# Batch norm with ReLU: two channels per partition in 8 KB rows, and parameters loaded as rows instead of columns

## Chip, cores and metric

The kernel runs on one core of a Trainium2 chip. The metric is the device time of one execution in microseconds (us); the median of several executions is given. The profile is one execution under the hardware profiler; its span is 1.8 to 2.2 us shorter than that execution's time, because the time also holds what lies outside the program's first and last record.

## The reference

```python
# x: (32, 128, 32, 32) float32; gamma, beta, running_mean, running_var: (128,)
normalized = (x - running_mean[None, :, None, None]) / np.sqrt(running_var[None, :, None, None] + eps)
scaled = normalized * gamma[None, :, None, None] + beta[None, :, None, None]
return np.maximum(scaled, 0).astype(np.float32)
```

Per channel this is `relu(scale * x + bias)` with scale = gamma / sqrt(var + eps) and bias = beta - mean * scale. The kernel reads 16.78 MB and writes 16.78 MB.

## The kernel before

Channels lie on the 128 partitions. An image's channel is 4 KB in a row in memory, so a tile of two images is a 1 MB transfer of 256 pieces of 4 KB. Loads are issued from SP, stores from ACT.

```python
x_r = x.rearrange("b c h w -> c b (h w)")
plan = [(b0, 2, 0, HW) for b0 in range(0, B - 2, 2)]
plan += [(B - 2, 1, 0, HW), (B - 1, 1, 0, HW // 2), (B - 1, 1, HW // 2, HW // 2)]
HEAD = 8; BUFS = 12
# ... the first 8 loads are issued from SP ...
nc.scalar.dma_start(out=var_t, in_=running_var.unsqueeze(1))   # [128, 1]: one 4-byte piece per partition
nc.scalar.dma_start(out=gamma_t, in_=gamma.unsqueeze(1))
nc.scalar.dma_start(out=mean_t, in_=running_mean.unsqueeze(1))
nc.scalar.dma_start(out=beta_t, in_=beta.unsqueeze(1))
# ... sqrt on ACT, four small operations on DVE give scale_t and bias_t ...
for k, (b0, nb, h0, nh) in enumerate(plan):
    # ... from k = 8 on, the tile's load is issued here ...
    nc.scalar.activation(out=xt, in_=xt, func=relu, bias=bias_t, scale=scale_t)
    nc.scalar.dma_start(out=out_r[:, b0 : b0 + nb, h0 : h0 + nh], in_=xt)
```

## Time and profile before

| | before |
|---|---|
| time, median (13 runs) | 87.54 us (87.38 to 87.67) |
| span of the profile | 85.8 us |
| plateau of the transfers, 24 to 66 us | 421 GB/s |
| mean rate, 1 to 10 us | 284 GB/s |
| first activation, first store issued | 11.85 us, 13.97 us |
| ACT busy | 35.1 us |

The DMA row counts tenths of busy time of the 16 DMA engines in each fortieth of the span; the GB/s row says what they moved. A stretch line gives the stretch, its length, the busy time of each engine with the number of instructions in brackets, the TensorE clock, the share of the DMA engines (just over 1.00 where packets overlap) and GB/s as the last number.

### The profile page before, as it was taken

What the parts mean: (1) busy time and instruction counts of PE and PEld (TensorE: products, weight loads), DVE (VectorE), ACT (ScalarE), POOL (GpSimd) and SP (SyncE); (2) the same over time, 40 slices, a digit from 0 to 9 for tenths busy, and PEclk for the clock granted to TensorE, in tenths of its full rate; (3) what the DMA queues carried; (4) which work ended last, traced back from release to release, by engine and by line L of the source; (5) the groups of instructions that cost most, each with busy time, mean ns of one, the idle gap of its engine ahead of it and who ended that gap; (6) DMA issues with size and microseconds to landing.
All of it is one profiled execution on the core that took longest, in us unless ns stands there. A gap on an engine that the chain in (4) does not pass through costs nothing.

```text
span 85.8 us, 137 instructions
## 1 busy us (share of the span) xinstructions
DVE 0.7 (1%) x5; ACT 35.1 (41%) x20; POOL 0.2 (0%) x4
## 2 busy tenths in 40 slices
DVE  0000100000000000000000000000000000000000
ACT  0024047979749500791000098000098497710000
POOL 0000000000000000000000000000000000000000
DMA  3899999999999999999999999999999999999991
GB/s 29 214 352 333 407 420 413 401 424 422 420 415 424 424 422 416 418 428 422 415 418 426 424 420 415 422 426 424 415 416 428 415 417 421 422 422 413 424 407 55
DMA packets 9600, 33.56 MB, mean 391 GB/s; under 512 B 1152, under 2 KB 1152, under 8 KB 9600
## 3 DMA queue, kind: packets, MB, share of 16 engines
q1 hardware_dynamic: 4512, 16.78, 49.7%
q10 hardware_dynamic: 5088, 16.78, 48.1%
HBM read 16.78 MB, written 16.78 MB: 391 GB/s over the span
## 4 chain that ended last, share of the span: by engine, by line
DMA 72%; ACT 10%; ACTq 4%; issue 1%; DVE 0%; SPq 0%; DVEq 0%
DMA out_dram<-xt 34%; DMA xt<-in_x_dram 27%; DMA beta_t<-in_beta_dram 11%; ACT xt L82 10%; ACTq L83 2%; ACTq L56 1%; ACTq L57 1%; ACTq L55 1%; DVE bias_t L74 0%; SPq L81 0%; DVEq L74 0%
## 5 line engine op out<-in xcount | busy, mean ns | idle before, releaser
L82 ACT ACTIVATE xt<-xt,bias_t,scale_t 128x2048 f32<-128x2048 f32 (+2 forms) x18 | 33.5, 1899 | 34.4 <-DMA out_dram<-xt 10.2
L64 ACT ACT_TABLE_LOAD x1 | 1.3, 1283 | 5.9 <-DMA var_t<-in_running_var_dram 5.9
L64 ACT ACTIVATE std_t<-var_t,eps_t 128x1 f32<-128x1 f32 x1 | 0.3, 295 | 0.0
L66 DVE RECIPROCAL rstd_t<-std_t 128x1 f32<-128x1 f32 x1 | 0.2, 163 | 6.6 <-ACT std_t L64 6.6
L74 DVE TENSOR_TENSOR bias_t<-beta_t,tmp_t 128x1 f32<-128x1 f32 x1 | 0.2, 159 | 1.4 <-DMA beta_t<-in_beta_dram 1.4
L73 DVE TENSOR_TENSOR tmp_t<-mean_t,scale_t 128x1 f32<-128x1 f32 x1 | 0.2, 160 | 1.2 <-DMA mean_t<-in_running_mean_dram 1.2
L69 DVE TENSOR_TENSOR scale_t<-gamma_t,rstd_t 128x1 f32<-128x1 f32 x1 | 0.2, 159 | 1.2 <-DMA gamma_t<-in_gamma_dram 1.2
L100 POOL MEMSET const-bfloat16-1.0<- 128x1 bf16 x1 | 0.1, 102 | 0.0
L100 POOL MEMSET const-uint8-127<- 128x1 uint8 x1 | 0.1, 102 | 0.0
L100 POOL MEMSET const-float32-0.0<- 128x1 f32 x1 | 0.1, 99 | 0.2 <-issue 0.2
L100 POOL MEMSET const-float32-1.0<- 128x1 f32 x1 | 0.1, 99 | 0.0
L61 DVE MEMSET eps_t<- 128x1 f32 x1 | 0.1, 59 | 0.8 <-PEq L100 0.8
## 6 DMA issues: line engine op xcount, KB each, us to landing
xt<-in_x_dram SPq DMA_DIRECT2D x15, 1024.0 KB, 16.4
out_dram<-xt ACTq DMA_DIRECT2D x15, 1024.0 KB, 12.2
xt<-in_x_dram SPq DMA_DIRECT2D x1, 512.0 KB, 22.3
xt<-in_x_dram SPq DMA_DIRECT2D x2, 256.0 KB, 19.4
out_dram<-xt ACTq DMA_DIRECT2D x1, 512.0 KB, 10.0
out_dram<-xt ACTq DMA_DIRECT2D x2, 256.0 KB, 9.6
var_t<-in_running_var_dram ACTq DMA_DIRECT2D x1, 0.5 KB, 5.1
gamma_t<-in_gamma_dram ACTq DMA_DIRECT2D x1, 0.5 KB, 7.5
```

Of the source, the lines that this page charges most:

```text
L55: nc.scalar.dma_start(out=var_t, in_=running_var.unsqueeze(1))
L56: nc.scalar.dma_start(out=gamma_t, in_=gamma.unsqueeze(1))
L57: nc.scalar.dma_start(out=mean_t, in_=running_mean.unsqueeze(1))
L61: nc.vector.memset(eps_t, eps_f)
L64: nc.scalar.activation(out=std_t, in_=var_t, func=sqrt, bias=eps_t, scale=1.0)
L66: nc.vector.reciprocal(out=rstd_t, in_=std_t)
L69: nc.vector.tensor_mul(out=scale_t, in0=gamma_t, in1=rstd_t)
L73: nc.vector.tensor_mul(out=tmp_t, in0=mean_t, in1=scale_t)
L74: nc.vector.tensor_sub(out=bias_t, in0=beta_t, in1=tmp_t)
L82: nc.scalar.activation(out=xt, in_=xt, func=relu, bias=bias_t, scale=scale_t)
L83: nc.scalar.dma_start(out=out_r[:, b0 : b0 + nb, h0 : h0 + nh], in_=xt)
L100: nc = _bacc.Bacc("TRN2", target_bir_lowering=False, num_devices=1)
```

## The change

It has two intents. First, longer pieces: the tensor is viewed flat, and each partition takes 2048 neighbouring elements, which are two channels of one image, so a 1 MB transfer is 128 pieces of 8 KB. A partition then holds two channels and needs two scale and bias columns. Second, cheaper parameters: each vector comes as one contiguous row on one partition, issued from GpSimd, and small matmuls against a single 1.0 turn even and odd elements into columns. Besides, all eight 2 MB tiles have a buffer of their own. The diff, cut to its core:

```diff
-    x_r = x.rearrange("b c h w -> c b (h w)")
+    x_p = x.rearrange("b c h w -> (b c h w)").rearrange("(j p f) -> p j f", p=C, f=F)   # F = 2 * HW
-    data = ctx.enter_context(tc.tile_pool(name="data", bufs=BUFS))
+    data = ctx.enter_context(tc.tile_pool(name="data", bufs=NT))                        # NT = 8 tiles of 2 MB
+        eng = nc.sync
+        eng.dma_start(out=tiles[k][:, h], in_=x_p[:, 2 * k + h])
-    nc.scalar.dma_start(out=var_t, in_=running_var.unsqueeze(1))      # and three more
+    for nm, src in (("g", gamma), ("b", beta), ("m", running_mean), ("v", running_var)):
+        r = consts.tile([1, C], fp32, name=f"r{nm}")
+        nc.gpsimd.dma_start(out=r, in_=src.unsqueeze(0))
+        for t in range(2):
+            rows[(nm, t)] = r[:, t : C : 2]
+        nc.tensor.matmul(out=p[0:C2], lhsT=r, rhs=ones1)              # for each of the eight rows
+        nc.tensor.matmul(out=p[C2:C], lhsT=r, rhs=ones1)
     # ... the constants' chain now runs twice, for t = 0 and 1 ...
-        nc.scalar.activation(out=xt, in_=xt, func=relu, bias=bias_t, scale=scale_t)
-        nc.scalar.dma_start(out=out_r[:, b0 : b0 + nb, h0 : h0 + nh], in_=xt)
+        for t in range(2):
+            nc.scalar.activation(out=xt[:, :, t * HW : (t + 1) * HW], in_=xt[:, :, t * HW : (t + 1) * HW],
+                                 func=relu, bias=bias_c[t], scale=scale_c[t])
+        for h in range(2):
+            seng = nc.scalar
+            seng.dma_start(out=out_p[:, 2 * k + h], in_=xt[:, h])
```

More of the change, by code (lines that the diff above doesn't have):

```diff
@@ L25 @@
     HW = H * W
-    assert C == nc.NUM_PARTITIONS, f"expected C == 128, got {C}"
-    x_r = x.rearrange("b c h w -> c b (h w)")
-    out_r = out.rearrange("b c h w -> c b (h w)")
+    C2 = C // 2
+    F = 2 * HW
+    x_p = x.rearrange("b c h w -> (b c h w)").rearrange("(j p f) -> p j f", p=C, f=F)
+    out_p = out.rearrange("b c h w -> (b c h w)").rearrange("(j p f) -> p j f", p=C, f=F)
+    g2 = gamma.rearrange("(cp t) -> t cp", t=2)
+    b2 = beta.rearrange("(cp t) -> t cp", t=2)
+    m2 = running_mean.rearrange("(cp t) -> t cp", t=2)
+    v2 = running_var.rearrange("(cp t) -> t cp", t=2)
     eps_f = float(eps)
@@ L34 @@
     sqrt = mybir.ActivationFunctionType.Sqrt
-    plan = [(b0, 2, 0, HW) for b0 in range(0, B - 2, 2)]
-    plan += [(B - 2, 1, 0, HW), (B - 1, 1, 0, HW // 2), (B - 1, 1, HW // 2, HW // 2)]
-    HEAD = 8
-    BUFS = 12
-    data = ctx.enter_context(tc.tile_pool(name="data", bufs=BUFS))
-    consts = ctx.enter_context(tc.tile_pool(name="consts", bufs=1))
-    head_tiles = []
-    for k in range(HEAD):
-        b0, nb, h0, nh = plan[k]
-        xt = data.tile([C, nb, nh], fp32, tag="xt")
-        head_tiles.append(xt)
-        nc.sync.dma_start(out=xt, in_=x_r[:, b0 : b0 + nb, h0 : h0 + nh])
@@ L51 @@
-    var_t = consts.tile([C, 1], fp32)
-    gamma_t = consts.tile([C, 1], fp32)
-    mean_t = consts.tile([C, 1], fp32)
-    beta_t = consts.tile([C, 1], fp32)
-    nc.scalar.dma_start(out=var_t, in_=running_var.unsqueeze(1))
-    nc.scalar.dma_start(out=gamma_t, in_=gamma.unsqueeze(1))
-    nc.scalar.dma_start(out=mean_t, in_=running_mean.unsqueeze(1))
-    nc.scalar.dma_start(out=beta_t, in_=beta.unsqueeze(1))
+    NB = 2
+    NT = B // (2 * NB)
+    data = ctx.enter_context(tc.tile_pool(name="data", bufs=NT))
@@ new lines, with b0, load @@
+    consts = ctx.enter_context(tc.tile_pool(name="consts", bufs=1))
+    ppool = ctx.enter_context(tc.tile_pool(name="ppool", bufs=1, space=bass.MemoryType.PSUM))
+    tiles = [data.tile([C, NB, F], fp32, name=f"xt{k}", tag="xt") for k in range(NT)]
+    def b0(k, h):
+        return (2 * k + h) * NB
+    def load(k, h):
+        eng = nc.sync
+        eng.dma_start(
+            out=tiles[k][:, h],
+            in_=x_p[:, 2 * k + h],
+        )
+    load(0, 0)
+    load(0, 1)
+    rows = {}
+    for nm, src in (("g", gamma), ("b", beta), ("m", running_mean), ("v", running_var)):
[3 more added lines that the diff above has]
+            rows[(nm, t)] = r[:, t : C : 2]
@@ L60 @@
+    load(1, 0)
+    load(1, 1)
+    for k in range(2, NT):
+        load(k, 0)
+        load(k, 1)
+    ones1 = consts.tile([1, 1], fp32)
+    nc.vector.memset(ones1, 1.0)
+    cols = {}
+    for key, r in rows.items():
+        p = ppool.tile([C, 1], fp32, name=f"p{key[0]}{key[1]}")
+        nc.tensor.matmul(out=p[0:C2], lhsT=r, rhs=ones1)
+        nc.tensor.matmul(out=p[C2:C], lhsT=r, rhs=ones1)
+        cols[key] = p
     eps_t = consts.tile([C, 1], fp32)
     nc.vector.memset(eps_t, eps_f)
-    std_t = consts.tile([C, 1], fp32)
@@ L64 @@
-    nc.scalar.activation(out=std_t, in_=var_t, func=sqrt, bias=eps_t, scale=1.0)
-    rstd_t = consts.tile([C, 1], fp32)
-    nc.vector.reciprocal(out=rstd_t, in_=std_t)
-    scale_t = consts.tile([C, 1], fp32)
-    nc.vector.tensor_mul(out=scale_t, in0=gamma_t, in1=rstd_t)
-    bias_t = consts.tile([C, 1], fp32)
-    tmp_t = consts.tile([C, 1], fp32)
-    nc.vector.tensor_mul(out=tmp_t, in0=mean_t, in1=scale_t)
-    nc.vector.tensor_sub(out=bias_t, in0=beta_t, in1=tmp_t)
-    for k, (b0, nb, h0, nh) in enumerate(plan):
-        if k < HEAD:
-            xt = head_tiles[k]
-        else:
-            xt = data.tile([C, nb, nh], fp32, tag="xt")
-            nc.sync.dma_start(out=xt, in_=x_r[:, b0 : b0 + nb, h0 : h0 + nh])
-        nc.scalar.activation(out=xt, in_=xt, func=relu, bias=bias_t, scale=scale_t)
-        nc.scalar.dma_start(out=out_r[:, b0 : b0 + nb, h0 : h0 + nh], in_=xt)
+    scale_c = {}
@@ new lines @@
+    bias_c = {}
+    for t in range(2):
+        std = consts.tile([C, 1], fp32, name=f"std{t}")
+        nc.scalar.activation(out=std, in_=cols[("v", t)], func=sqrt, bias=eps_t, scale=1.0)
+        rstd = consts.tile([C, 1], fp32, name=f"rstd{t}")
+        nc.vector.reciprocal(out=rstd, in_=std)
+        sc = consts.tile([C, 1], fp32, name=f"sc{t}")
+        nc.vector.tensor_mul(out=sc, in0=cols[("g", t)], in1=rstd)
+        tmp = consts.tile([C, 1], fp32, name=f"tmp{t}")
+        nc.vector.tensor_mul(out=tmp, in0=cols[("m", t)], in1=sc)
+        bi = consts.tile([C, 1], fp32, name=f"bi{t}")
+        nc.vector.tensor_sub(out=bi, in0=cols[("b", t)], in1=tmp)
+        scale_c[t] = sc
+        bias_c[t] = bi
@@ new lines @@
+    for k in range(NT):
+        xt = tiles[k]
+        for t in range(2):
+            nc.scalar.activation(
+                out=xt[:, :, t * HW : (t + 1) * HW],
+                in_=xt[:, :, t * HW : (t + 1) * HW],
+                func=relu,
+                bias=bias_c[t],
+                scale=scale_c[t],
+            )
+        for h in range(2):
+            seng = nc.scalar
+            seng.dma_start(
+                out=out_p[:, 2 * k + h],
+                in_=xt[:, h],
+            )
```

## The prediction

> **What bounds the kernel now.** I read the page's first two parts first, then the stretches, then the waits. Engine work is small: the busiest engine is ACT with 35.1 us of 85.8. The DMA row is at nine tenths in all slices but the first two and the last.
>
> ```profile
> span 85.8 us, 137 instructions
> DVE 0.7 (1%) x5; ACT 35.1 (41%) x20; POOL 0.2 (0%) x4
> ...
> DMA  3899999999999999999999999999999999999991
> GB/s 29 214 352 333 407 420 413 401 424 422 420 415 424 424 422 416 418 428 422 415 418 426 424 420 415 422 426 424 415 416 428 415 417 421 422 422 413 424 407 55
> DMA packets 9600, 33.56 MB, mean 391 GB/s; under 512 B 1152, under 2 KB 1152, under 8 KB 9600
> ```
>
> The reader is to see a plateau near 421 GB/s, a ragged start (29, 214, 352, 333), and a short end (55). The stretches (columns: stretch, length, DVE, ACT, POOL, clock, DMA share, GB/s) give these in numbers.
>
> ```profile
> 1.00:10.00 9.00, 0.32 (x2) 1.58 (x2) 0.00 (x0) 1.00 0.89 284
> ...
> 24.00:66.00 42.00, 0.00 (x0) 16.27 (x8) 0.00 (x0) 1.00 1.03 421
> ```
>
> All bytes at the plateau rate are 33.55 MB / 421 GB/s = 79.7 us. The span is 85.8, so 6.1 us are lost at the two ends. At the start, 284 GB/s x 9 us = 2.56 MB have moved by 10.0 us, which would take 6.1 us at 421: 3.9 us lost. At the end some 2.2 us remain: the last bytes move near 84.0 us, and the rest is the landing of the last store. The kernel is therefore a DMA stream, and only three things can shorten it: the plateau rate, the start, the end.
>
> The start in half-microsecond stretches:
>
> ```profile
> 1.50:2.00 0.50, 0.00 (x0) 0.00 (x0) 0.00 (x0) 1.00 1.44 115
> 2.00:2.50 0.50, 0.00 (x0) 0.00 (x0) 0.00 (x0) 1.00 0.13 16
> 2.50:3.00 0.50, 0.00 (x0) 0.00 (x0) 0.00 (x0) 1.00 0.80 295
> 3.00:3.50 0.50, 0.00 (x0) 0.00 (x0) 0.00 (x0) 1.00 1.02 344
> 3.50:4.00 0.50, 0.00 (x0) 0.00 (x0) 0.00 (x0) 1.00 1.17 180
> 4.00:4.50 0.50, 0.00 (x0) 0.00 (x0) 0.00 (x0) 1.00 0.69 164
> ...
> 7.50:8.00 0.50, 0.15 (x1) 0.00 (x0) 0.00 (x0) 1.00 0.81 295
> ```
>
> The loads begin to flow at about 2.4 us (first issue at 0.73 us). That part is latency and stays. After it the rate should be flat, but it falls to 180 and 164 at 4 us and to about 300 near 7.5 us, while the four parameter vectors are under way. They land 5.1 (variance), 7.5, 8.3 and 9.3 us after their issue, as the DMA issues show, though each is 0.5 KB. From 2.5 to 10.0 us 2.49 MB moved, worth 5.9 us of 7.5: the dips cost 1.6 us. The load queue's own waits add that issues of x tiles wait for those vectors:
>
> ```profile
> SPq L49 <- DMA var_t<-in_running_var_dram: 3.6, 1, 3.6
> SPq L49 <- DMA mean_t<-in_running_mean_dram: 2.9, 1, 2.9
> ```
>
> No data dependence explains this, so I read it as transfers of all queues taking turns in a small set of completion counters. The first store leaves at 13.97 us, but from 10 to 14 us the loads alone already give 419 GB/s, so a late first store costs nothing.
>
> **What the Trainium skill says.** All four places are in the page "DMA: Bandwidth & Descriptors".
> (1) Section "Where 436 GB/s comes from": 16 ports of 32 B at 850 MHz give 435.2 GB/s. The trace agrees: its plateau of 421 is 97% of that, so at most 2.5 us of 79.7 can come from the rate.
> (2) Section "Why small descriptors are slow (HBM only)": a fixed overhead of about 3 cycles per packet. For 4 KB that is 131 cycles for 128, or 425 GB/s; for 8 KB 259 for 256, or 430: an estimate of +1.2%. The trace agrees in direction: the last two stores have rows of 2 KB, and from 82.5 to 83.5 us, where they drain, the rate is 381 and 410, mean 395.
> (3) Section "Specifications": pieces under 512 B make the DMA read, modify and write. The trace has 1152 such packets. 640 are one completion on each of 16 engines for 40 transfers; the other 512 are the four vectors, one element per partition. The dips stand where these are queued, which agrees; the trace does not show their cause.
> (4) Section "Anatomy of one DMA — SWDGE (gpsimd) path": about 2.0 us fixed for a transfer issued by GpSimd. No such transfer is in this trace.
>
> **The change part by part.**
> *Rows of 8 KB.* Two neighbouring channels of one image now go to one partition, so a 1 MB transfer is 128 rows of 8 KB in place of 256 of 4 KB. The bytes are unchanged and so is the number of 1 MB transfers, apart from the 512 and 256 KB ones at the end, which become one. Per engine a 4 KB packet takes 4096 / (421/16) = 155.7 ns, a 2 KB one 2048 / (395/16) = 83.0 ns. The line through the two is 10 ns per packet plus 72.7 ns per 2 KB, which makes 301 ns for 8 KB, or 435 GB/s: the skill's ceiling, so surely too much. Its own overhead gives 421 x 1.012 = 426. I take the middle of 421 and 435: 428 GB/s, hence 33.55 / 428 = 78.4 us, 1.3 us saved. All of it is on the path, because the stream is the path.
>
> *Parameters.* The four column loads on the ACT queue become four contiguous 512 B rows from GpSimd, so 512 four-byte pieces go. Of the 1.6 us that the dips cost I expect 1.2 us back; something will be left of it, since four small transfers and the first big ones still compete. New beside it: 16 small matmuls which turn the rows into columns, a doubled constant chain (two square roots, ten DVE operations of 0.16 us instead of four: about 1 us more), all beside loads that run anyway. An estimate for the first activation: four GpSimd issues of some 1 us, 2 us to land, 0.5 us of matmul, 1.28 us table load, 0.3 us square root and some 1 us of DVE, so about 10 us against 11.85 now. Neither is on the path.
>
> *ACT.* 15 activations of 2048 elements (2.09 us) and three smaller become 16 of two strided pieces of 1024, about 16 x 2.09 = 33.4 us, against 33.5 now. Sixteen store issues of 0.38 us add 6.1. ACT needs 39.5 us of 80.
>
> *Buffers.* Eight tiles of 2 MB hold the whole input, so no load needs a buffer that a store has to free. Before, loads waited long for stores, but the stream stayed at 421, so removing this wait is worth nothing by itself. The tile of 2 MB delays the first store by one activation, which also costs nothing.
>
> *Sum.* 87.5 - 1.3 (rate) - 1.2 (start) = 85.0 us. The end keeps its 2.2 us.
>
> **The rivals.**
> (a) *The rows don't matter*: the hardware cuts them to 4 KB or the plateau is bound elsewhere. For: 421 is already close to the ceiling. Against: the 2 KB stretch is slower, and single packets seem to follow the row length. It makes 87.5 - 1.2 = 86.3 us, within 2%.
> (b) *The start doesn't improve*: the dips belong to the first loads, or the GpSimd transfers bring their own delay. For: the dip at 4 us also falls where only the first three loads had been issued. Against: tiny packets are queued just there. It makes 86.2.
> (c) *ACT or the counters become the bound.* With 2 MB per step, ACT gives 2 MB in 2 x 2.09 + 2 x 0.38 = 4.9 us, and stores alone drain 2 MB in 5.0 us. If loads finish first with nothing computed ahead, small gaps appear. Transfers that take turns in shared counters can also hold a load behind a store. Against: before, the last activation ended at 75.4 us with 8 us of stores still queued, and ACT has 40 us to spare; constants could come some 25 us later without an effect. With a gap of 2 to 3 us it makes 87 to 88.
> (d) *Both gains at full size*: 435 GB/s and all of the dips: 87.5 - 2.5 - 1.6 = 83.4.
>
> **Range and chances.** Two per cent faster is 85.76 us. The middle estimate of 85.0 lies 0.8 us below it; either gain failing alone puts the time just above, 86.2 to 86.3. I give both gains about two in three of arriving at near their size or one at more than it. The range 83.5 to 86.9 us goes from (d) to a case where one fails and a small gap appears. Slower needs both to fail and (c) to cost over 4 us: 0.03.
>
> **What would show it.** Right: about half as many data packets (4096, beside the small ones); a plateau of 426 to 430 in the stretches; no dips to 180 after 2.5 us, so over 2.8 MB moved by 10 us; no parameter landing later than about 8 us; DMA at nine tenths to the end; ACT idle for half of the time. Wrong: a plateau of 421 with 8 KB rows breaks the first step; dips at the same places without the column loads break the second; slices under nine tenths in the middle, ended by waits for a landing or for ACT, would make (c) true.

## More of the kernel before

```profile
10.00:16.00 6.00, 0.32 (x2) 3.67 (x2) 0.00 (x0) 1.00 1.03 414
16.00:22.00 6.00, 0.00 (x0) 5.54 (x4) 0.00 (x0) 1.00 1.02 417
```

Both are close to the plateau: in this kernel the stores join without a visible loss.

## The result

| | before | after |
|---|---|---|
| time, median | 87.54 us (13 runs) | 85.36 us (8 runs, 85.04 to 85.68) |
| span of the profile | 85.8 us | 83.5 us |
| plateau, 24 to 66 us | 421 GB/s | 428 GB/s |
| 1 to 10 us | 284 GB/s | 355 GB/s |
| 10 to 16, 16 to 22 us | 414, 417 GB/s | 427, 365 GB/s |
| first activation, first store issued | 11.85, 13.97 us | 10.34, 14.45 us |

The ratio is 0.9752 (95% interval 0.9737 to 0.9768), so the kernel is faster by 2.5%. A ratio is the mean time of one kernel's runs over the mean of the other's runs in the same rounds; it is not quite the ratio of the medians in the table. Executions over 1.5% slower than the fastest of the same kernel are left out of the means. In a second set of rounds (e1 below) the same kernel had 0.9799: this kernel's advantage is known to about half a per cent only, and the second set alone would not settle whether it passes 2%.

The page of the changed kernel, parts 1 to 3:

```profile
span 83.5 us, 191 instructions
...
DMA  4799999999999999999999999999999999999992
GB/s 63 294 424 409 432 420 432 408 318 397 408 424 440 436 424 420 424 432 436 424 420 424 432 436 424 424 420 432 436 432 428 408 432 436 436 424 412 428 436 98
DMA packets 4736, 33.56 MB, mean 402 GB/s; under 512 B 640, under 2 KB 640, under 8 KB 640
```

There are 4736 packets where 9600 were. 640 are small, so 4096 are data packets of 8 KB: the hardware does not cut the rows. The ragged start is shorter. But slices nine and ten now read 318 and 397, where before had 424 and 422, and the DMA row shows nine tenths there all the same. Its stretches (a PE and a PEld column now stand ahead of DVE):

```profile
1.00:10.00 9.00, 2.19 (x32) 1.97 (x32) 0.59 (x5) 1.74 (x3) 2.06 (x4) 1.00 0.93 355
10.00:16.00 6.00, 0.00 (x0) 0.00 (x0) 0.43 (x4) 4.67 (x3) 0.00 (x0) 1.00 1.01 427
16.00:22.00 6.00, 0.00 (x0) 0.00 (x0) 0.00 (x0) 5.47 (x3) 0.00 (x0) 1.00 0.96 365
24.00:66.00 42.00, 0.00 (x0) 0.00 (x0) 0.00 (x0) 18.52 (x9) 0.00 (x0) 1.00 1.01 428
```

The start gains and the plateau gains, as predicted. The third line is new: from 16 to 22 us the engines are busy for 0.96 of the time but move only 365 GB/s. They mostly do not wait for work: single packets take longer. At its worst a half microsecond moves 279:

```profile
17.00:17.50 0.50, 0.00 (x0) 0.00 (x0) 0.00 (x0) 0.50 (x2) 0.00 (x0) 1.00 0.89 279
```

The first store is issued at 14.45 us, so the dip begins some 2 us after it. The trace also keeps each packet's start, length and size (the views print only their sums). By these records the load packets from 16 to 22 us take 358 ns on average and up to 721, where they take 309 from 24 to 66 us; the store packets take 309 as ever. The slow load packets start at 16.4 us, and the first store packet only at 18.3 us: 36 of the 56 that are more than a tenth too long start before it (in e3, further down, 58 of 59). So the dip follows the issue of the first store, but for the most part no stored byte moves yet. "When stores join" stands for this stretch from here on.

Where the time went, in microseconds of the plateau rate (lost = length - length x rate / plateau). Rate: 33.55 MB at 428 instead of 421 GB/s, 79.7 - 78.4 = 1.3 us gained. From 1 to 10 us: before lost 9 x (1 - 284/421) = 2.9, after 9 x (1 - 355/428) = 1.5; 1.4 us gained. From 10 to 22 us: before lost 0.16, after 6 x (1 - 427/428) + 6 x (1 - 365/428) = 0.90; 0.7 us given back. That makes 2.0 us of the 2.3 by which the span is shorter; the other 0.3 us was not taken apart.

### The profile page after: what moved, and what is told of

Read it like the earlier page. It is cut to its first block, busy times and chain, and to the rows that moved or that the text cites. A ratio compares the mean times of both kernels' runs of the same rounds, so it can differ in the third digit from the quotient of the medians.

```text
span 83.5 us, 191 instructions
## 1 busy us (share of the span) xinstructions
PE 2.2 (3%) x32; PEld 2.0 (2%) x32; DVE 1.1 (1%) x10; ACT 34.5 (41%) x19; POOL 2.3 (3%) x8
## 2 busy tenths in 40 slices
DMA packets 4736, 33.56 MB, mean 402 GB/s; under 512 B 640, under 2 KB 640, under 8 KB 640
## 3 DMA queue, kind: packets, MB, share of 16 engines
q1 hardware_dynamic: 2304, 16.78, 49.2%
q10 hardware_dynamic: 2304, 16.78, 47.6%
## 4 chain that ended last, share of the span: by engine, by line
DMA 70%; ACT 8%; issue 3%; POOL 1%; ACTq 1%; PE 1%; DVE 1%; POOLq 0%
DMA xt<-in_x_dram 46%; DMA out_dram<-xt 18%; ACT xt L108 8%; DMA rm<-in_running_mean_dram 7%; ACTq L117 1%; POOL rg L65 1%; PE pm L82 1%; ACT std L93 1%; POOL rb L65 1%; DVE tmp L99 0%; DVE sc L97 0%; PE pv L82 0%; DVE bi L101 0%; PE pv L83 0%; DVE rstd L95 0%
## 5 line engine op out<-in xcount | busy, mean ns | idle before, releaser
L108 ACT ACTIVATE xt<-xt,bi,sc 128x2048 f32<-128x2048 f32 x16 | 32.7, 2088 | 29.5 <-DMA xt<-in_x_dram 19.9
L82 PE MATMUL pg<-ones,rg 1*64 1x1 f32 x4 | 0.6, 239 | 6.7 <-DMA rg<-in_gamma_dram 6.7
L82 PEld LDWEIGHTS pg<-ones,rg 1*64 1x64 f32 x4 | 0.5, 210 | 6.7 <-issue 6.7
L65 POOL DMA_DIRECT2D rg<-in_gamma_dram x1 | 0.6, 619 | 0.8 <-POOLq L137 0.8
L82 PE MATMUL pb<-ones,rb 1*64 1x1 f32 x4 | 0.6, 246 | 0.3 <-DMA rb<-in_beta_dram 0.3
L83 PE MATMUL pb<-ones,rb 1*64 1x1 f32 x4 | 0.6, 246 | 0.0
L82 PE MATMUL pm<-ones,rm 1*64 1x1 f32 x4 | 0.6, 246 | 0.1
L83 PE MATMUL pg<-ones,rg 1*64 1x1 f32 x4 | 0.6, 246 | 0.0
L83 PE MATMUL pm<-ones,rm 1*64 1x1 f32 x4 | 0.6, 246 | 0.0
L82 PE MATMUL pv<-ones,rv 1*64 1x1 f32 x4 | 0.6, 240 | 0.0
L83 PE MATMUL pv<-ones,rv 1*64 1x1 f32 x4 | 0.6, 240 | 0.0
L82 PEld LDWEIGHTS pv<-ones,rv 1*64 1x64 f32 x4 | 0.5, 219 | 0.0
L83 PEld LDWEIGHTS pv<-ones,rv 1*64 1x64 f32 x4 | 0.5, 219 | 0.0
L82 PEld LDWEIGHTS pb<-ones,rb 1*64 1x64 f32 x4 | 0.5, 209 | 0.3 <-DMA rb<-in_beta_dram 0.3
L82 PEld LDWEIGHTS pm<-ones,rm 1*64 1x64 f32 x4 | 0.5, 208 | 0.2 <-DMA rm<-in_running_mean_dram 0.2
L83 PEld LDWEIGHTS pb<-ones,rb 1*64 1x64 f32 x4 | 0.5, 209 | 0.0
L83 PEld LDWEIGHTS pm<-ones,rm 1*64 1x64 f32 x4 | 0.5, 208 | 0.0
L83 PEld LDWEIGHTS pg<-ones,rg 1*64 1x64 f32 x4 | 0.5, 208 | 0.0
```

Of the source, the lines that this page charges most:

```text
L65: nc.gpsimd.dma_start(out=r, in_=src.unsqueeze(0))
L82: nc.tensor.matmul(out=p[0:C2], lhsT=r, rhs=ones1)
L83: nc.tensor.matmul(out=p[C2:C], lhsT=r, rhs=ones1)
L108: nc.scalar.activation(out=xt[:, :, t * HW : (t + 1) * HW], in_=xt[:, :, t * HW : (t + 1) * HW], func=relu, bias=bias_c[t], scale=scale_c[t],)
```

## The experiments

All runs gave correct results, each timed in five rounds beside the kernel before; the runs of one set share those rounds. Sets: e1 to e4, e5 to e8, e9 to e11, e12. The table gives what the stretches say. "Start" is the mean rate from 1 to 10 us with the time lost in it, "stores join" the time lost from 10 to 22 us, both against that kernel's plateau.

| kernel | time us (ratio to before) | plateau | start GB/s (lost us) | stores join, lost us |
|---|---|---|---|---|
| before | 87.54 | 421 | 284 (2.9) | 0.16 |
| after | 85.36 (0.9752) | 428 | 355 (1.5) | 0.90 |
| e1 after, again | 85.69 (0.9799) | 428 | 346 (1.7) | 0.93 |
| e2 four columns added | 86.62 (0.9914) | 428 | 295 (2.8) | 0.15 |
| e3 before, parameters only | 87.12 (0.9961) | 421 | 340 (1.7) | 0.90 |
| e4 after, 4 KB pieces | 87.04 (0.9956) | 421 | 329 (2.0) | 0.81 |
| e5 rows from ACT | 85.90 (0.9808) | 428 | 358 (1.5) | 1.12 |
| e6 one row more from ACT | 86.04 (0.9824) | 427 | 338 (1.9) | 0.72 |
| e7 one late transfer from ACT | 85.87 (0.9810) | 427 | 348 (1.7) | 0.77 |
| e8 stores from SP | 85.13 (0.9717) | 425 | 350 (1.6) | 0.04 |
| e9 one column added, ACT | 86.12 (0.9837) | 428 | 295 (2.8) | -0.06 |
| e10 second load from ACT | 85.34 (0.9751) | 428 | 360 (1.4) | 0.79 |
| e11 four columns added, GpSimd | 86.41 (0.9897) | 427 | 278 (3.1) | 0.10 |
| e12 16 KB pieces | 86.62 (0.9893) | 432 (66 to 80 us) | 353 (1.6) | 0.13 |

The plateau is that of 24 to 66 us, except for e12. For e8, the losses of the first ten microseconds and of the joining are against 428 GB/s, the plateau of the same pieces in e1; for e12 they are against its 66 to 80 us, as its 24 to 66 us hold a dip of their own. In those two the stores come behind all loads, near 42 us, so their last column shows loads alone.

### e1: the changed kernel again

No edit.

> The changed kernel unaltered, for a second profile and as the yardstick of this round: 85.4 us, ratio 0.975. In the first profile the rate fell to 279-344 GB/s from 16.5 to 19.5 us, worth 0.9 us, just before the first store's packets move. If this dip belongs to the kernel (stores joining the loads), it stands at the same place again. If it is a disturbance of one execution, it is elsewhere or gone, and that profile's span is some 0.9 us shorter.

85.69 us, and its stretches from 10 to 22 us:

```profile
10.00:16.00 6.00, 0.00 (x0) 0.00 (x0) 0.73 (x7) 4.34 (x3) 0.00 (x0) 1.00 1.00 423
16.00:22.00 6.00, 0.00 (x0) 0.00 (x0) 0.00 (x0) 5.80 (x3) 0.00 (x0) 1.00 1.01 367
```

The dip is back at the same place with the same size. It belongs to the kernel.

### e2: the column loads put back beside the rows

```diff
+    for nm, src in (("v", running_var), ("g", gamma), ("m", running_mean), ("b", beta)):
+        extra = consts.tile([C, 1], fp32, name=f"col{nm}")
+        nc.scalar.dma_start(out=extra, in_=src.unsqueeze(1))
```

> The changed kernel with the four column loads of before put back on the ACT queue beside the new row loads; their results are not used, so only their traffic is added. Theory (column loads make the dips of the start): dips to under 200 GB/s return near 4 us, 1 to 10 us falls from 355 to near 290 GB/s, time +1.2 to +1.5 us, 86.6 to 86.9 us. Rival (the dips came from the 4 KB rows or from the first loads alone): 85.4 us, the start stays at 350 or more.

86.62 us, 0.93 us more than e1 in the same rounds. The mean of the first ten microseconds fell as expected (without dips under 200 near 4 us: after 3 us the lowest half microsecond moves 246), but the last line was not expected by anybody:

```profile
1.00:10.00 9.00, 2.06 (x30) 1.85 (x32) 0.00 (x0) 1.28 (x1) 2.05 (x4) 1.00 0.81 295
...
16.00:22.00 6.00, 0.00 (x0) 0.00 (x0) 0.00 (x0) 5.52 (x3) 0.00 (x0) 1.00 1.02 427
```

So the columns do slow the start (295 against 346 in e1, 1.1 us), and with them the dip at the first stores is gone (427 against 367, 0.8 us). Of the 0.93 us that the time grew, the two together explain 0.3. The span of the profile grew by only 0.5 us (84.4 against 83.9), so some 0.4 us lie outside the program's records; the rest the stretches do not show.

### e3: the kernel before with only its parameters changed

```diff
-    nc.scalar.dma_start(out=var_t, in_=running_var.unsqueeze(1))      # and three more
+    for nm, src in (("g", gamma), ("b", beta), ("m", running_mean), ("v", running_var)):
+        r = consts.tile([1, C], fp32, name=f"r{nm}")
+        nc.gpsimd.dma_start(out=r, in_=src.unsqueeze(0))
+        p = ppool.tile([C, 1], fp32, name=f"p{nm}")
+        nc.tensor.matmul(out=p, lhsT=r, rhs=ones1)
```

> The kernel before with only its parameters changed: contiguous rows from GpSimd and four matmuls in place of the four column loads; 4 KB rows and the plan of transfers stay. Theory (two separate gains, 1.3 us of rate and 1.5 us of start): plateau stays 421 GB/s, start gains 1.5 us: 86.0 us. Rival (the start gains nothing without 8 KB rows): 87.5 us.

87.12 us, only 0.33 below before: neither theory. The start did gain, and the gain was lost again:

```profile
1.00:10.00 9.00, 1.99 (x8) 1.85 (x8) 0.35 (x3) 1.53 (x2) 2.05 (x4) 1.00 0.91 340
10.00:16.00 6.00, 0.00 (x0) 0.00 (x0) 0.29 (x2) 5.18 (x3) 0.00 (x0) 1.00 1.02 382
16.00:22.00 6.00, 0.00 (x0) 0.00 (x0) 0.00 (x0) 5.54 (x4) 0.00 (x0) 1.00 1.00 397
```

Its first store is issued at 12.48 us, earlier than in e1, and the dip came earlier with it: it straddles 16 us and costs 0.90 us, against 0.16 in before. The pieces are 4 KB here, so 8 KB rows are not what makes the dip.

### e4: the changed kernel in 4 KB pieces

```diff
-    tiles = [data.tile([C, NB, F], fp32, name=f"xt{k}", tag="xt") for k in range(NT)]
+    tiles = [data.tile([C, 2, NB, HW], fp32, name=f"xt{k}", tag="xt") for k in range(NT)]
-            out=tiles[k][:, h],
-            in_=x_p[:, 2 * k + h],
+            out=tiles[k][:, :, h],
+            in_=x_p[:, 2 * k + h].rearrange("p (t f) -> p t f", t=2),
```

The activations and stores follow the same layout.

> The changed kernel with the tile laid out so that the two channels of an image are not neighbours on a partition: the same addresses in memory, the same 1 MB transfers and order, but pieces of 4 KB. Theory (a fixed cost per packet sets the rate): 8192 data packets, plateau back from 428 to 421 GB/s, time +1.3 us, 86.7 us. Rival (the rate comes from the new order of addresses or from the free buffers): plateau 428, 85.4 us.

87.04 us, 1.35 us more than e1. Packets and plateau:

```profile
DMA packets 8832, 33.56 MB, mean 394 GB/s; under 512 B 640, under 2 KB 640, under 8 KB 8832
...
24.00:66.00 42.00, 0.00 (x0) 0.00 (x0) 0.00 (x0) 18.51 (x9) 0.00 (x0) 1.00 1.03 421
```

Same addresses, order and buffers, twice as many packets: the plateau is back at 421. The theory stands, with its size: 1.3 us expected, 1.35 measured (the two intervals leave about 0.2 us either way).

### e5, e6, e7: is the dip the first use of ACT's queue?

In before and e2 ACT issues the columns at the start; in the kernels with a dip ACT issues nothing before the first store. So a new theory: the first use of ACT's DMA queue disturbs the stream. Three edits use that queue earlier:

```diff
 e5: the four rows from ACT
-        nc.gpsimd.dma_start(out=r, in_=src.unsqueeze(0))
+        nc.scalar.dma_start(out=r, in_=src.unsqueeze(0))
 e6: one unused row more, from ACT, at the start
+    early = consts.tile([1, C], fp32, name="early")
+    nc.scalar.dma_start(out=early, in_=gamma.unsqueeze(0))
 e7: one small transfer from ACT that waits for the last row (8.7 us)
+    late = consts.tile([1, C], fp32, name="late")
+    nc.scalar.dma_start(out=late, in_=rv)
```

> The changed kernel with its four parameter rows issued from ACT in place of GpSimd. Theory (the first use of ACT's DMA queue disturbs the loads that run for some 3 us, wherever it falls; the changed kernel moved it from the start, where the stream is not yet up, to the first store, where it costs 0.9 to 1.0 us): no dip from 16 to 20 us, first 10 us at 340 or more since only 16 pieces of 32 B per row go, time 84.5 to 84.8 us. Rival (the dip belongs to the first stores, or to loads in flight): the dip stays, 85.6 us.

> The changed kernel with one more 512 B row load, unused, issued from ACT at the start. Theory (first use of ACT's queue): one such transfer is enough, no dip when the stores start, 84.5 to 84.8 us. Rival (first stores): nothing changes, 85.6 us. If e5 gains and this doesn't, it is not the first use but the GpSimd transfers that make the dip.

> The changed kernel with one small transfer from ACT that waits for the last parameter row, so ACT's queue is first used near 8.5 us, in the middle of the loads and 6 us before the first store. Theory: the dip of some 0.4 MB moves to about 10 to 14 us, none at 16 to 20, time as the changed kernel's, 85.4 to 85.7 us. Rival (first stores): the dip stays at its place after the first store's issue.

85.90, 86.04 and 85.87 us: no gain in any of them, and the dip stayed, 1.12, 0.72 and 0.77 us. In e7 the loads run undisturbed after the early use, 426 GB/s from 10 to 16 us, and dip only when stores are issued:

```profile
10.00:16.00 6.00, 0.00 (x0) 0.00 (x0) 1.03 (x8) 5.17 (x5) 0.00 (x0) 1.00 1.02 426
16.00:22.00 6.00, 0.00 (x0) 0.00 (x0) 0.00 (x0) 4.99 (x4) 0.00 (x0) 1.00 1.02 373
```

The test has a hole. ACT's queue in e6 shows 2306 packets, two more than the 2304 of e1, a data piece and its completion, so it seems that only one of the 16 engines was touched; e5 shows 2312, so one piece per row and not the 16 that its theory counted on; e7 shows 2336, that is one piece and one completion on each of the 16:

```profile
q10 hardware_dynamic: 2306, 16.78, 47.1%
```

The theory could be saved as "the first transfer on that queue with many pieces per engine". That is what e9 to e11 test.

### e8: stores from SP

```diff
-            seng = nc.scalar
+            seng = nc.sync
```

> The changed kernel with its stores issued from SP behind all loads, so that ACT issues no transfer at all and stores begin only when the loads are done. Theory: no dip of 0.4 MB anywhere before 40 us, and none where the stores begin, as SP's queue is long in use: 84.5 us, if one queue keeps the stream as full as two. Rival (first stores): a dip of 0.9 us where stores begin, 85.6 us or more.

85.13 us, ratio 0.9717 (0.9693 to 0.9742), the lowest. SP issues all loads first, so stores move only when the loads are through. The dip is gone:

```profile
10.00:16.00 6.00, 0.00 (x0) 0.00 (x0) 0.63 (x6) 5.44 (x3) 0.00 (x0) 1.00 1.02 430
16.00:22.00 6.00, 0.00 (x0) 0.00 (x0) 0.00 (x0) 6.00 (x4) 0.00 (x0) 1.00 1.01 423
24.00:66.00 42.00, 0.00 (x0) 0.00 (x0) 0.00 (x0) 19.71 (x10) 0.00 (x0) 1.00 1.01 425
```

The gain is smaller than the 0.9 us of the dip, as the plateau is 425 instead of 428 (422 from 24 to 40 us, where only loads move; 428 from 44 to 66 us, where only stores do). This run avoids the meeting of running loads with stores almost altogether, so it doesn't tell the queue from the stores. It was timed in other rounds than e1; against the changed kernel's 0.9752 and 0.9799 it is likely the better kernel, but the two were not run side by side.

### e9, e10, e11: which earlier transfer takes the dip away?

```diff
 e9: one unused column, 128 pieces of 4 B, from ACT
+    early = consts.tile([C, 1], fp32, name="early")
+    nc.scalar.dma_start(out=early, in_=gamma.unsqueeze(1))
 e10: the second 1 MB load from ACT
-        eng = nc.sync
+        eng = nc.scalar if (k, h) == (0, 1) else nc.sync
 e11: the four unused columns of e2, from GpSimd
-        nc.scalar.dma_start(out=extra, in_=src.unsqueeze(1))
+        nc.gpsimd.dma_start(out=extra, in_=src.unsqueeze(1))
```

> The changed kernel with one unused column load (128 pieces of 4 B, eight on each engine) issued from ACT at the start. New theory, since one piece on one engine or on each engine did not help: the dip belongs to the first transfer on ACT's queue that has many pieces per engine, and the four column loads of before took it at the start. Then no dip, or a much smaller one, from 16 to 20 us, and the first 10 us lose some of it: 300 to 340 GB/s, time 85.0 to 85.9 us. Rival (only large stores, or all four columns, matter): dip of 0.9 us unchanged, time 85.9 us or more.

> The changed kernel with its second 1 MB load issued from ACT: no traffic added, ACT's queue is in full use from the start. New theory: no dip where the stores begin, start at 340 GB/s or more, 84.6 to 85.0 us. Rival (stores joining from a second queue make the dip, whatever it did before): dip unchanged, 85.6 us.

> The changed kernel with the same four unused column loads as in e2, issued from GpSimd. It has the 512 small pieces, but ACT's queue is not used before the first store and no counter of the loads is taken. If the small pieces themselves slow the loads: first 10 us near 295 to 310 GB/s and the dip at the stores stays, 86.6 us. If the start of e2 was lost to ACT's queue and to the counters: start near 345, dip at the stores stays, 85.7 us.

e9, 86.12 us: one column is enough to slow the start, and no dip follows.

```profile
1.00:10.00 9.00, 1.80 (x28) 1.66 (x30) 0.00 (x0) 1.28 (x1) 2.05 (x4) 1.00 0.85 295
...
16.00:22.00 6.00, 0.00 (x0) 0.00 (x0) 0.00 (x0) 5.45 (x3) 0.00 (x0) 1.00 1.02 433
```

e10, 85.34 us: a full 1 MB load has gone through ACT's queue early, and the dip is there all the same.

```profile
1.00:10.00 9.00, 2.31 (x32) 2.04 (x32) 0.00 (x0) 1.41 (x2) 2.05 (x4) 1.00 0.91 360
...
16.00:22.00 6.00, 0.00 (x0) 0.00 (x0) 0.00 (x0) 5.80 (x3) 0.00 (x0) 1.00 0.99 373
```

e11, 86.41 us (four runs from 86.35 to 87.12; two more, at 88.09, were slow): ACT issues nothing before its first store at 19.11 us, and there is no dip, neither to 22 us nor from 22 to 28 us, where the rate is 430 GB/s. The start is the slowest of all:

```profile
1.00:10.00 9.00, 0.00 (x0) 0.00 (x0) 0.00 (x0) 1.26 (x1) 4.20 (x8) 1.00 0.80 278
...
16.00:22.00 6.00, 0.00 (x0) 0.00 (x0) 0.00 (x0) 5.00 (x3) 0.00 (x0) 1.00 1.00 419
```

Two theories fall here. It is not the first use of ACT's queue: with it early (e10) the dip stays, without it (e11) the dip is missing. It is not simply stores that join loads: in before, e2, e9 and e11 they join without a loss, and not one load packet is more than a tenth too long there between the first store's issue and the next ten microseconds. What the fourteen profiles do show is a rule without a mechanism. All four kernels that load a column (before, e2, e9, e11) lose 2.8 to 3.1 us in the start and at most 0.16 when stores join. All eight profiles without a column whose stores join running loads (seven kernels, as after and e1 are the same) lose 1.4 to 2.0 us in the start and 0.7 to 1.1 when stores join. The two whose stores come behind all loads lose 1.6 us in the start; where their stores begin, from 40 to 44 us, e8 loses 0.1 us (418 GB/s) and e12 0.4 (389). It looks as if one disturbance came once, either with the first column or with the first stores; e8, which shows it nowhere, does not fit that picture. What the issue of the first store sets off in the loads before its own data moves was not tested.

### e12: 16 KB pieces, stores from SP

```diff
-    F = 2 * HW                       # two channels per partition, 1 MB transfers
+    F = 4 * HW                       # four channels per partition, 2 MB transfers
-        nc.tensor.matmul(out=p[0:C2], lhsT=r, rhs=ones1)
-        nc.tensor.matmul(out=p[C2:C], lhsT=r, rhs=ones1)
+        for i in range(G):           # G = 4, for each of four columns
+            nc.tensor.matmul(out=p[CG * i : CG * (i + 1), t : t + 1], lhsT=r[:, t:C:G], rhs=ones1)
-            seng = nc.scalar
+            seng = nc.sync
```

> A version meant to beat both kernels: stores from SP behind all loads as in e8, and four neighbouring channels per partition, so 2 MB transfers of 128 pieces of 16 KB, with four activations of 1024 elements for each tile. Theory (a fixed time per packet): a 4 KB piece took 155.7 ns per engine at 421 GB/s and an 8 KB one 306.2 ns at 428, so 5.2 ns are fixed and 16 KB take 607 ns, 432 GB/s, 0.7 us less than e8: 84.4 us, 2048 data packets. Rival (pieces are cut at 8 KB, or 428 is a ceiling of its own): 85.1 us. No dip of 0.4 MB in either case.

86.62 us: the version missed. Yet late in the kernel its rate is what the fixed time per packet foretold, and the loss is elsewhere (queues and kinds of the page, then stretches):

```profile
q1 hardware_dynamic: 2304, 33.56, 94.1%
q0 software_dynamic: 128, 0.00, 0.1%
q8 instruction: 1, 0.02, 0.1%
```

```profile
24.00:66.00 42.00, 0.00 (x0) 0.00 (x0) 0.00 (x0) 25.33 (x23) 0.00 (x0) 1.00 1.01 426
40.00:44.00 4.00, 0.00 (x0) 0.00 (x0) 0.00 (x0) 4.00 (x5) 0.00 (x0) 1.00 1.00 389
66.00:80.00 14.00, 0.00 (x0) 0.00 (x0) 0.00 (x0) 0.00 (x0) 0.00 (x0) 1.00 1.01 432
81.00:82.00 1.00, 0.00 (x0) 0.00 (x0) 0.00 (x0) 0.00 (x0) 0.00 (x0) 1.00 0.08 33
82.00:83.00 1.00, 0.00 (x0) 0.00 (x0) 0.00 (x0) 0.00 (x0) 0.00 (x0) 1.00 0.08 33
```

From 24 to 66 us the mean is only 426 GB/s, in good part because of the dip near 42 us, where its stores follow its loads. From 66 to 80 us it is 432, where e8 has 427 with 8 KB pieces and before and e4 have 420 and 421 with 4 KB; a 16 KB packet takes 611 ns in the records. Then from 81 to 83 us the rate is 33, about what one of 16 engines moves alone (432 / 16 = 27). The packet records bear this out: the last three data packets run one after the other, 607 ns apart, and end 1.8 us after all others. So fifteen engines have finished, one trails, and the last store waits for it.

The first of the three queue lines makes 2048 data packets; the third shows a fetch of instructions of 0.02 MB in one packet, which no other kernel here has in the middle of its stream (this program has 377 instructions against 191). It took 0.96 us, from 13.8 us on. The loads land 4.9 us apart by the trace, except twice, when it is 6.0: across this fetch (13.4 to 19.3 us) and across the dip near 42 us (38.9 to 44.9 us). These two delays, 1.1 us each, together exceed the trail of 1.8. An estimate from them: the fetch made about half of the trail and the dip the rest, if both fell on the same engine, which the records do not name. It was not tested.

## Why the prediction was right

The time, 85.36 us, lies inside the range and 0.4 us above the estimate; "faster by over 2%" came true, in the second set of rounds only just (2.0%, interval 1.9 to 2.2). The number is better than its terms: of the two gains, one was hit by taking the middle of an interval, and the other was too large. By its steps:

**What bounds the kernel.** Right. Between before and after, the bytes at the plateau rate, the start and the dip account for 2.0 of the 2.3 us by which the spans differ.

**Rows of 8 KB, 1.3 us.** Right in mechanism: 4096 packets of 8 KB, and e4 gives 1.35 us for this part alone. That the size came out so well, 428 GB/s as taken, has luck in it: it was the middle of two estimates, the line through the 2 KB stretch (435) and the fixed overhead of the Trainium skill (426; page "DMA: Bandwidth & Descriptors", section "Why small descriptors are slow (HBM only)"). At 428 GB/s an 8 KB packet takes 8192 B / (428/16) = 306.2 ns per engine, 150.5 more than the 155.7 of a 4 KB packet, so 5.2 ns are fixed per packet, and 432 GB/s at 16 KB agrees. So the line's 10 ns were twice the real figure: at 5.2 + 75.2 ns a 2 KB packet would make 407 GB/s, and the stretch it took them from moved 395, with some 4 KB packets in it and with the stream near its end. Rival (a) is refuted. (Its bound on what the rate can give, 2.5 us, should be 79.7 - 33.55 / 435.2 = 2.6.)

**Parameters, 1.2 us.** The start did lose its dips: 1.4 us by the profile of after, 1.2 by that of e1, so as a statement on the first ten microseconds it was right. But as a term of the sum the step failed. It took what the start gains as gained for good, and its sum has no term for the moment when the stores join: from "a late first store costs nothing" it went over to first stores that cost nothing. e3, which makes this part of the change alone, gained 0.33 us. The stream loses 0.9 us when the first stores join, which the kernel before does not (0.16). So the term of 1.2 us was mis-sized; net of the dip it is 0.3 (e3) to 0.7 (stretches of after). Its signs for this step in the rates came true, 3.2 MB by 10 us and no half microsecond at 180 after 2.5 us, but all of them look at the start alone.

**Why pieces of 4 B.** The prediction blamed 512 small pieces, in line with what the page's section "Specifications" says on pieces under 512 B. The columns do slow running loads, also from another queue (e2, e9, e11). But in the start one column costs as much as four (295 GB/s in both e9 and e2, spans of 84.3 and 84.4 us; e2's time is 0.5 us longer than e9's, but it was timed in other rounds and most of that lies outside the span), so the number of pieces doesn't seem to be the measure. Nor do the pieces fill the engines: in the packet records each takes 9 ns, 512 of them 0.3 us of the 16 engines' time. Why a column slows the start, and why it takes the later dip away, is open.

**ACT, buffers, the chain of constants.** Right, as far as the profile shows, that none is on the path: ACT is busy for 41% of the span, and the plateau holds. Loads still wait for stores, 21.5 us in sum in the load queue's waits against 27.4 before, though each has a buffer of its own. The trace bears out the prediction's reading here: in both kernels all loads and stores signal their landing through the same eight completion counters in turn (before, the four columns too; after, the rows have four others). The plateau of 428 stands beside these waits. (Its "ten DVE operations instead of four" counts two that set constants; the chain has eight instead of four.) The first activation came at 10.34 us (10 estimated), though by another sum: the table load ran at 0.98 us, ahead of the wait, a GpSimd issue took 0.5 us and not 1, and the rows landed later than assumed:

```profile
rg<-in_gamma_dram POOLq DMA_DIRECT2D x1, 0.5 KB, 5.3
```

**What made it come out.** Taking each part by itself, rows gave 1.35 us (e4 against e1) and parameters 0.33 (e3 against before), 1.7 of the 2.0 us that the mean of the two ratios, 0.978, stands for. The rest was not taken apart; the 2 KB pieces of before, which are gone, are worth at most 1.05 MB x (1/395 - 1/421) = 0.16 us. So the sum of 2.5 us came within 0.5 of what was measured, although one of its two terms kept only between a quarter and three fifths of its size.

## What to carry to other kernels

Where a stream of transfers is the bound, give each piece 8 KB rather than 4: it was worth 1.35 us of 87 here and is read from the packet count and the plateau. A gain at the start of such a stream is only kept if nothing later takes it back, so compare the rate in stretches to the end and not only where the change acts; e3 gained 1.2 us by 10 us and kept 0.3. Keeping stores behind the loads, where memory on the core holds the whole input, avoided most of the dip with 8 KB pieces (e8), less so with 16 KB (e12); and before going to longer pieces yet, look at the last two microseconds for a single engine that trails.

## What the Trainium skill lacked or had wrong

- Page "DMA: Bandwidth & Descriptors", section "Why small descriptors are slow (HBM only)": it names a fixed time per packet, but of joining descriptors into packets it says that this pays only up to 256 B, and it has nothing on longer pieces. For plain rows, longer is still faster far above that: 421, 428 and 432 GB/s at 4, 8 and 16 KB.
- The same page, section "Anatomy of one DMA — SWDGE (gpsimd) path": about 2.0 us fixed, called constant. Beside running loads the four 512 B rows from GpSimd landed 5.3 to 5.8 us after issue.
- The same page, section "Specifications", has the rule of 512 B but not what small pieces do to others: one 0.5 KB column of 4 B pieces (e9) came with 295 GB/s over 9 us where e1 had 346, and four columns (e2) came with 295 too.
- No page has the dip that follows the issue of the first store beside running loads: 0.7 to 1.1 us in eight profiles, absent in four kernels that loaded a column before.
- The same page says only in passing, in its section on the iDMA fabric, that a bulk load runs at the pace of its slowest engine. No page says what one delayed engine costs a stream at its end: in e12 one trailed by 1.8 us (33 GB/s), in a program that also fetched 0.02 MB of instructions in mid-stream.
